# One step of an RWKV-7 and convolution layer: group norms with the tokens on the partitions, key norms folded into the scores, low-rank products on quarters of the array, the samples' convolution on TensorE, and the sample unit two places forward

## The chip, the cores and the metric

The kernel runs on one core of one Trainium2 chip. The metric is the device time of one execution in microseconds. Three executions were timed, and their median is the time of a kernel; one more was recorded by the profiler, and the views of the profile come from that one.

## What is computed

One layer over a prompt of 1024 tokens and over 8 samples of 4 tokens each, width 1024. Half of the mixing width goes through a recurrent branch (8 heads of 64), half through a causal convolution of 31 taps. Both read one input projection and end in one output projection. Cut to what matters here:

```python
h = _rms_norm(x, g_pre) * (1 + scale) + shift            # 1024 wide
u = h @ w_in                                             # r k v g w_lo a_lo | glu_a glu_b g_c
u_r = u_r + (u_prev - u_r) * mu                          # mix with the token before
w_log = -softplus(-(w0 + tanh(w_lo) @ w_up)) - 0.5       # low rank, 64 -> 512
a     = sigmoid(a0 + a_lo @ a_up)                        # low rank, 64 -> 512
kk = heads(k * k_k);  kk = kk / max(sqrt(sum(kk**2)), 1e-12)   # per token and head
# per token:  S = S diag(decay) - (S kk)(kk * a)^T + v k^T ;  y = S r
y   = group_norm(y, 8 heads)                             # 64 channels a group, per token
y_r = (y + bonus) * silu(g_r)
glu  = glu_a * sigmoid(glu_b)
conv = depthwise(concat(state_conv, glu), 31 taps) + b_dw
y_c  = silu(group_norm(conv, 8 groups)) * silu(g_c)
x + gate * _rms_norm(concat(y_r, y_c) @ w_out, g_post)
```

The states after the last token (recurrent, shift and convolution) are outputs too. The samples go through the same mathematics from given states.

## The kernel before

**Layout.** Between the projections everything lies with channels on the 128 partitions (two heads or two groups of 64) and tokens along the free dimension. The input projection runs in blocks of 128 output channels by 256 tokens: each is 8 slices of the contraction by three products in float32r (high part by high part, high by low, low by high), 24 instructions that write a tile `ps`. The output projection is the same with tiles `po`: 8 token blocks, each in two halves of 24 products (`JOBS`), the first half for the convolution's channels, the second for the recurrent branch's.

**Units.** The recurrent branch works in units of four heads (two channel blocks) by 128 tokens (256 columns): 16 units of the prompt, (0,0) to (1,7), and one of the samples (`SMP`). `ORDER` lists them. In a unit, `keys_unit` forms the low-rank products `zw` and `za` and the squares of the keys, `keys_unit2` norms the keys, `scores_unit` forms the products of queries and keys (`ap`), `blocks`, `solve`, `inverse` invert a small triangular matrix, `chain_unit` carries the state (tiles `cb`, `Yp`), `post_unit` norms the result. `chain_sample` and `post_sample` do this for the samples. The convolution branch goes by pieces of 128 channels by 256 tokens, 16 in all: `glu`, `shifts`, `convolutions` (tile `cv`), `post_conv`.

**The norms.** `inverse_norms` serves keys and both group norms. Two products (tile `n`, named `n2` in the code) sum the squares with the tokens on the partitions; VectorE applies the guard, GpSimd takes the power -1/2, ScalarE and GpSimd split it in two parts (`nR`, `nS`), two products turn it back (`n<-cs,nS`), ScalarE copies it (`nT`), and one product (`bc`) spreads it over the channels, where VectorE multiplies. A group norm has one product more ahead of this, which subtracts the mean (`yc`). So there are 17 norms of keys, 17 of the units' results and 16 of the convolution: 50 in all, 33 of them with `yc`.

**The samples' convolution** (`sample_block`) was four products over the taps per channel block on GpSimd, each summed by VectorE.

**What sets the order.** The whole program is recorded as strands and put into one order when it is built: `_Schedule.run` takes at each step the operation that can start first by a table of estimated costs (`_cost`), with the rank of its strand as tie break. On the chip each engine then works through its list in that order; SyncE (`Z`) issues nearly all DMAs, in its own list. `PLAN` sets the order of the projection's blocks (a lower case letter is the first half of the tokens, an upper case one the second). PSUM has six banks for most tiles: at most three of them (`room["pj"]`, `PJ = 3`) for `ps`, and at most four (`room["rest"]`) for all others, among them two for a `po` pair whose block number is not a multiple of three.

**The output weights** (`output_weights`) take the room that the normalised input had (`ha`, `hb`): the tiles `wo` are loaded, rounded by ScalarE and the rest is formed by GpSimd. `mixes` does the same with the mixed channels (`raw`, `mh`, `ml`).

Of the kernel before, what the change touches and what calls it, by code (L numbers as in the profile page):

```python
# [38 lines left out]
B1 A1 V2 A2 c0+ A3 g0+ c3 c1 g3 B3 C2 g2 G2 g1 C1 G1 G3 C3"""  # L39
# [11 lines left out]
ORDER = [(0, 0), (0, 1), (0, 2), (0, 3), (1, 0), (1, 1), (1, 2), (1, 3), (0, 4), (0, 5), (0, 6), (0, 7), (1, 4), (1, 5), (1, 6), (1, 7), SMP]  # L51
# [17 lines left out]
P_WDW = 57  # L69
P_GPRE = P_WDW + 4 * TAPS  # L70
# [237 lines left out]
class _Engine:  # L308
# [38 lines left out]
    def _cost(self, op, a, k):  # L347
# [3 lines left out]
        if self._n == "PE":  # L351
# [6 lines left out]
            if K == m == 64 and n == 128:  # L358
                return 0.065
            if a[1].dtype == F32R:  # L360
                return max(0.107, n * 0.00045)
# [43 lines left out]
def hymba_step(ctx, tc, xp, xs, cT, ssT, w_ada, badag, gpost, w_in, wup, par, cst, wkv, cvs, w_out, wdd,  # L405
# [14 lines left out]
    accd = tc.dram_tile([4, 128, 32], F32, name="accd")  # L420
    gld = [tc.dram_tile([128, 30 + SEQ], F32, name=f"gld{j}") for j in range(4)]
# [14 lines left out]
    hw = pr[:, P_WDW:P_WDW + 4 * TAPS]  # L436
    nR = const.tile([128, 19], F32, name="nR")
    half = nR[:, 18:19]
# [7 lines left out]
    heads4 = const.tile([68, 128], F32R, name="heads4")  # L446
# [8 lines left out]
    for i in range(3):  # L455
        for h in range(2):
            r, a = slice(32 * i, 32 * i + 4), C_ID + 32 * i + h
            V.tensor_tensor(heads4[r, 64 * h:64 * h + 64], cs[r, a:a + 1].to_broadcast([4, 64]),
                            cs[r, a + 2:a + 3].to_broadcast([4, 64]), ALU.add)
# [4 lines left out]
    sl = _Slots({"raw": 2, "ga": 2, "whi": WB, "wlo": WB, "qa": 4, "kb": 2, "unit": 2, "wd": 2, "sh": 2, "wa": 8, "ts": 1, "d2": 2, "dt": 1, "ti": 2}, sched)  # L464
# [79 lines left out]
    def modulation():  # L544
# [13 lines left out]
        for j in range(4):  # L558
# [3 lines left out]
            for i in range(KT // 2):  # L562
# [11 lines left out]
                if i == 1 and j == 0:  # L574
# [7 lines left out]
                    V.tensor_scalar(hw, hw, 0.5, None, ALU.mult)  # L582
# [227 lines left out]
    def output_weights():  # L810
        woh, wol = op["woh"], op["wol"] = {}, {}
        for ph in range(2):
            yield from wait(("proj", ph))
# [4 lines left out]
            jobs = [(4 - 4 * ph + k, q) for k in range(4) for q in range(2)]  # L818
            loaded, todo = [], jobs[:]
            for k, q in jobs:  # L820
                for tag in ("ga", "raw")[:1 + ph]:
                    while todo and sl.live[tag] < sl.bufs[tag]:
                        k_, q_ = todo.pop(0)
                        yield from sl.need(tag)
                        w = wp.tile([128, 512], F32, tag=tag, name="wo", bufs=sl.bufs[tag])
                        Z.dma_start(out=w, in_=w_out[k_ * 128:(k_ + 1) * 128, 512 * q_:512 * q_ + 512])
                        loaded.append((tag, w))
                if not loaded:
                    k_, q_ = todo.pop(0)
                    yield from sl.need("ga")  # L830
                    w = wp.tile([128, 512], F32, tag="ga", name="wo", bufs=sl.bufs["ga"])
                    Z.dma_start(out=w, in_=w_out[k_ * 128:(k_ + 1) * 128, 512 * q_:512 * q_ + 512])
                    loaded.append(("ga", w))
# [3 lines left out]
                G.tensor_tensor(wol[k][:, cc], w, woh[k][:, cc].bitcast(F32), ALU.subtract)  # L837
# [10 lines left out]
    def mixes():  # L848
        yield from wait("weights")
        for i, q in JOBS:  # L850
# [8 lines left out]
            G.tensor_tensor(ml, raw, mh.bitcast(F32), ALU.subtract)  # L859
# [107 lines left out]
    def gate(x, p, g, t):  # L967

        keys = [("z", ("c", p), g)] if x == "c" else [("z", p // 2, 2 * g), ("z", p // 2, 2 * g + 1)]
        n = UN + 32 * (x == "c" and g == NU - 1)  # L970
# [81 lines left out]
    def proj_conv(j):  # L1052
# [15 lines left out]
        def ev_c(g, ps, t):  # L1068
            for o, x in parts(t, ps, g):
                S.activation(o, x, AF.Tanh, scale=0.5)  # L1070
                V.scalar_tensor_tensor(o, o, 1.0, x, ALU.add, ALU.mult)
            gate("c", j, g, t)
# [28 lines left out]
    nT = cp1.tile([128, 288], F32R, name="nT")  # L1101
# [4 lines left out]
    def inverse_norms(nn, n, how, guard):  # L1106

        while not norms:
            yield BLOCK
# [700 lines left out]
    def taps_sample():  # L1810
        for j, ph in halves_of("ba"):
            if ph:
                yield from sample_block(j)
# [264 lines left out]
```

## Time and profile before

| | |
|---|---|
| timed executions | 866.39, 866.58 and 872.11 us; median 866.58 us |
| the profiled execution | 874.14 us, its span 872.4 us |
| TensorE busy | 815.5 us of the span |
| VectorE, ScalarE, GpSimd busy | 417.3, 462.8, 402.5 us |
| mean granted TensorE clock | 0.975 |

A span is the time from the first to the last instruction of the profiled execution. Most operations are recorded by one helper, so that the program's line says little (it is L341 nearly everywhere) and groups are told apart by the names of their tiles: `n<-cs,nS` writes tile `n` from `cs` and `nS`. A product in float32 is two instructions in the trace (x2), one in float32r is one. "PE" is the matrix product, "PEld" the load of its stationary operand. Busy time of a group of products is the union of spans that overlap, so what a product takes from the engine is better read as the distance from its start to that of the next instruction.

### The profile page before, as it was taken

How to read it: one execution, taken by the hardware profiler on the slowest of the kernel's cores; microseconds unless marked ns; L12 is line 12 of the kernel's file. 1: busy time of each engine (PE TensorE's matmuls, PEld its weight loads, DVE VectorE, ACT ScalarE, POOL GpSimd, SP SyncE). 2: the span in 40 equal slices, each digit the busy share in tenths (PEclk: the TensorE clock that was granted, in tenths of full speed). 3: DMA queues.
4: the chain of work that ended last, by engine and by line, in shares of the span. 5: the costliest groups of instructions: out<-in, count | busy, mean ns of one | idle time of the engine just before them, and what ended most of it. 6: DMA issues, size and time to landing. Idle time of an engine off the chain costs nothing.

```text
span 872.4 us, 23611 instructions
## 1 busy us (share of the span) xinstructions
PE 815.5 (93%) x9050; PEld 666.9 (76%) x9050; DVE 417.3 (48%) x1012; ACT 462.8 (53%) x1276; POOL 402.5 (46%) x759
## 2 busy tenths in 40 slices
PE   4868999999999999999999999999999999599995
PEld 2647888897889778888789878788987997475763
DVE  4556443562455554562662655574766363113122
ACT  4447577556676366672584567576655564211201
POOL 3237456463447216234325343644753765534332
PEclk9999899999999999999999999999999999698998
DMA  9987889788546753438735736435693676765432
GB/s 322 314 271 242 278 295 323 226 268 251 165 129 207 184 152 114 137 110 247 208 105 171 235 100 201 135 123 184 210 296 110 194 225 184 210 224 193 156 121 85
DMA packets 147729, 172.38 MB, mean 198 GB/s; under 512 B 23296, under 2 KB 105600, under 8 KB 147616
## 3 DMA queue, kind: packets, MB, share of 16 engines
q1 hardware_dynamic: 147328, 170.28, 63.0%
q8 instruction: 71, 1.16, 0.6%
q10 hardware_dynamic: 288, 0.59, 0.2%
q14 instruction: 42, 0.34, 0.1%
HBM read 112.68 MB, written 58.13 MB: 196 GB/s over the span
## 4 chain that ended last, share of the span: by engine, by line
PE 69%; DMA 14%; DVE 5%; ACT 4%; POOL 3%; issue 3%; SPq 1%; POOLq 0%; DVEq 0%; ACTq 0%
PE ps L341 30%; PE po L341 8%; PE cv L341 6%; PE n L341 4%; PE cb L341 4%; DMA wa<-w_ada 3%; PE ap L341 3%; PE Yp L341 2%; DMA xt<-xp 2%; PE yc L341 2%; PE p L341 2%; SPq L341 1%; PE bc L341 1%; DMA wd<-wdd 1%; ACT arena L341 1%
## 5 line engine op out<-in xcount | busy, mean ns | idle before, releaser
L341 PE MATMUL ps<-hb,whi 128*128 128x258 f32 (+3 forms) x928 | 199.0, 301 | 0.0
L341 PE MATMUL ps<-ha,whi 128*128 128x256 f32 (+2 forms) x864 | 180.9, 301 | 4.3 <-ACT ha L341 3.2
L341 PEld LDWEIGHTS ps<-hb,whi 128*128 128x128 f32 x928 | 149.6, 189 | 6.3 <-issue 2.7
L341 PEld LDWEIGHTS ps<-ha,whi 128*128 128x128 f32 x864 | 138.5, 191 | 14.8 <-issue 4.0
L341 PE MATMUL ps<-hb,wlo 128*128 128x258 f32 (+3 forms) x464 | 140.1, 302 | 0.0
L341 PE MATMUL ps<-ha,wlo 128*128 128x256 f32 (+2 forms) x432 | 130.9, 303 | 2.4 <-POOL wlo L341 2.4
L341 POOL TENSOR_TENSOR wlo<-raw,whi 128x512 fp32r<-128x512 f32 x58 | 78.4, 1352 | 66.1 <-ACT whi L341 50.2
L341 POOL TENSOR_TENSOR nR<-nR 128x4 f32<-128x4 f32 (+2 forms) x56 | 55.8, 998 | 77.5 <-DVE nR L341 77.2
L341 PEld LDWEIGHTS ps<-hb,wlo 128*128 128x128 f32 x464 | 87.6, 189 | 3.4 <-issue 1.2
L341 PEld LDWEIGHTS ps<-ha,wlo 128*128 128x128 f32 x432 | 82.4, 191 | 7.6 <-POOL wlo L341 3.0
L341 PE MATMUL cv<-SH,wd 128*32 128x256 f32 x1024 | 61.7, 389 | 4.0 <-DMA kept<-wlo 2.2
L341 ACT ACTIVATE arena<-ps,hp 128x256 f32<-128x256 f32 (+3 forms) x72 | 32.2, 455 | 51.7 <-PE ps L341 45.5
L341 ACT ACTIVATE X<-AB,cs 32x64 f32<-32x64 f32 x136 | 54.7, 403 | 2.1
L341 PEld LDWEIGHTS cv<-SH,wd 128*32 128x32 f32 x1024 | 35.1, 112 | 23.5 <-issue 2.7
L341 DVE SCALAR_TENSOR_TENSOR arena<-arena 128x256 f32<-128x256 f32 (+1 forms) x64 | 33.6, 527 | 34.3 <-DMA arena<-prj_a 13.1
L341 DVE TENSOR_TENSOR arena<-arena,bc 128x256 f32<-128x256 f32 (+2 forms) x50 | 20.6, 414 | 58.7 <-PE bc L341 56.2
L341 POOL TENSOR_TENSOR Ti<-Ti,tm 128x15 f32<-128x15 f32 (+4 forms) x135 | 41.1, 304 | 8.8
L341 ACT ACTIVATE whi<-raw 128x512 fp32r<-128x512 f32 x58 | 36.3, 626 | 15.6 <-DMA raw<-w_in 11.2
L341 POOL TENSOR_TENSOR tm<-D,Ti 128x15 f32<-128x15 f32 (+4 forms) x135 | 39.5, 293 | 10.2 <-DVE D L341 1.2
L341 ACT ACTIVATE arena<-arena 128x256 f32<-128x256 f32 (+3 forms) x100 | 41.1, 415 | 2.8 <-DVE ec L341 0.6
L341 DVE SCALAR_TENSOR_TENSOR arena<-ps,pr,arena 128x256 f32<-128x256 f32 (+4 forms) x40 | 17.5, 441 | 50.4 <-ACT arena L341 50.0
L341 POOL TENSOR_TENSOR arena<-arena,mx 128x256 f32<-128x256 f32 (+2 forms) x32 | 25.1, 785 | 35.3 <-ACT mx L341 31.8
(204 smaller groups left out, 1652.4 us busy)
## 6 DMA issues: line engine op xcount, KB each, us to landing
whi<-kept SPq DMA_DIRECT2D x52, 256.0 KB, 3.0
wlo<-kept SPq DMA_DIRECT2D x52, 256.0 KB, 3.8
raw<-w_in SPq DMA_DIRECT2D x50, 256.0 KB, 3.8
kept<-whi SPq DMA_DIRECT2D x44, 256.0 KB, 3.4
kept<-wlo SPq DMA_DIRECT2D x44, 256.0 KB, 3.2
wa<-w_ada SPq DMA_DIRECT2D x32, 256.0 KB, 5.4
SH<-gld SPq DMA_DIRECT2D x48, 142.0 KB, 4.0
xt<-xp SPq DMA_DIRECT2D x8, 512.0 KB, 5.4
```

The source lines that it names most:

```text
L341: emit = lambda: f(*a, **k)
```

## The change

- **Group norms in token layout.** `group_norm` turns the tile by `T.transpose` (tile `tp`, one per 128 tokens), so that the tokens lie on the partitions. VectorE sums each group, divides by 64, subtracts; ScalarE squares; VectorE sums; GpSimd adds the guard, takes the power and multiplies; two more transposes turn it back (tile `yc`). The products `yc` with `bcen`, `n` and `bc` are gone.
- **Key norms.** `square_sums` forms the sum of squares of each key with the keys' position on the partitions: eight products of a 64x64 stationary operand and one column (`n<-cs,arena 64x1`). The keys are no longer multiplied. Instead the reciprocal of the square norm (`inv`) goes into the scores' first half (`AB`, on VectorE, where ScalarE copied it before) and into `MV` in `chain_unit` and `chain_sample`: there one instruction of ScalarE over 64x128 becomes two over 64x64, each with a scale per partition, and VectorE multiplies by a tensor instead of by -1.
- **Low-rank products on quarters.** `zw` and `za` of the prompt's units: four products of 64x128 stationary operands become eight of 64x64, each with its place in the array.
- **The samples' convolution on TensorE.** `glu_sample` writes the samples' columns to memory, `shifts` loads them four times shifted and `convolutions` runs 32 products of 32 columns per channel block, with the weights of the prompt's last piece. `post_conv_sample` norms and gates all four blocks at once. The products over the taps on GpSimd and their sums on VectorE are gone, as are the weights for them (`hw`).
- **Order.** `SMP` stands two places ahead of the end in `ORDER`; `B3` three places further ahead in `PLAN`.
- **Output weights.** The loads of the second half may start once the last weights are in, ahead of the last projection; every second low part of that half, and all `ml`, are formed by VectorE instead of GpSimd.
- Two of the planner's estimated costs are raised a little.

```diff
-B1 A1 V2 A2 c0+ A3 g0+ c3 c1 g3 B3 C2 g2 G2 g1 C1 G1 G3 C3"""
+B1 A1 V2 A2 c0+ A3 B3 g0+ c3 c1 g3 C2 g2 G2 g1 C1 G1 G3 C3"""
-ORDER = [..., (1, 4), (1, 5), (1, 6), (1, 7), SMP]
+ORDER = [..., (1, 4), (1, 5), SMP, (1, 6), (1, 7)]
...
+    def square_sums(nn):
+        n2 = yield from bank([128, NCH], "n2")
+        for u in range(NCH):
+            for h in range(2):
+                T.matmul(n2[H[h], u:u + 1], nn[H[h], 64 * u:64 * u + 64], cs[H[h], C_ONE + 64 * h:C_ONE + 64 * h + 1],
...
+        V.tensor_scalar(t, n2, 1e-24, None, ALU.max)
...
+            for a in range(2):
+                w = slice(128 * i + 64 * a, 128 * i + 64 * a + 64)
+                for x, z in enumerate((zw, za)):
+                    T.matmul(z[H[a], cc], wu[H[x], w], tw[H[x], c0:c0 + 128], start=True, stop=True, tile_position=(64 * x, 64 * a))
...
-                S.activation(AB[H[h], :, 0, :], aps[h][H[h], :, 0:64], AF.Copy)
+                V.tensor_tensor(AB[H[h], :, 0, :], aps[h][H[h], :, 0:64], iv(h), ALU.mult)
...
-            S.activation(mv[H[0], :, c, 0, :], cb[H[0], 1], AF.Copy, scale=-1.0)
-            V.tensor_scalar(mv[H[1], :, c, 1, :], cb[H[1], 1], -1.0, None, ALU.mult)
+            for i, u in slots:
+                S.activation(MV[H[0], u, 0, :], cb[H[0], 1, i], AF.Copy, scale=inv[H[0], i, c:c + 1])
+            V.tensor_tensor(mv[H[1], :, c, 1, :], cb[H[1], 1], inv[H[1], :, c].unsqueeze(2).to_broadcast([64, 2, 64]), ALU.mult)
...
     def group_norm(src, n, guard):
-        T.matmul(yc[:, :n], bcen, src, start=True, stop=True)
...
-        bc = yield from inverse_norms(q, n, ALU.add, guard)
-        V.tensor_tensor(q[:, :n], src, bc[:, :n], ALU.mult)
...
+        for i, w in tiles:
+            T.transpose(tp[0:w, i, :], src[:, 128 * i:128 * i + w], ident)
...
+            V.tensor_reduce(a, by_group(tp, ii, w), mybir.AxisListType.X, ALU.add)
+            V.tensor_scalar(a, a, 1.0 / 64, None, ALU.mult)
+            V.tensor_tensor(by_group(qv, ii, w), by_group(tp, ii, w), spread(a), ALU.subtract)
+            S.activation(sq[0:w, ii], qv[0:w, ii], AF.Square, scale=0.125)
+            V.tensor_reduce(b, by_group(sq, ii, w), mybir.AxisListType.X, ALU.add)
+            G.tensor_scalar(b, b, 1.0, guard, ALU.mult, ALU.add)
+            G.tensor_tensor(b, b, half[0:w].unsqueeze(2).to_broadcast([w, m, 2]), ALU.pow)
+            G.tensor_tensor(by_group(qv, ii, w), by_group(qv, ii, w), spread(b), ALU.mult)
...
+        for i, w in tiles:
+            T.transpose(yc[:, 128 * i:128 * i + w], qv[0:w, i, :], ident[0:w, 0:w])
...
-            G.tensor_tensor(ml, raw, mh.bitcast(F32), ALU.subtract)
+            V.tensor_tensor(ml, raw, mh.bitcast(F32), ALU.subtract)
-                G.tensor_tensor(wol[k][:, cc], w, woh[k][:, cc].bitcast(F32), ALU.subtract)
+                (V if ph and q else G).tensor_tensor(wol[k][:, cc], w, woh[k][:, cc].bitcast(F32), ALU.subtract)
...
+                x = sh[:, :, 4 * m:4 * m + UN]
+                if g == NU:
+                    x = sh[:, :, 0:NB * 34].rearrange("p c (b x) -> p c b x", x=34)[:, :, :, 4 * m:4 * m + 4]
```

What this moves on the engines is shown at three places.

TensorE in the first third of the program, before: a norm's last products (`n<-cs,nS`, then `bc`) around a convolution, the low-rank product `zw` with its stationary operand of 128 columns, and the mean's product `yc` of another norm.

```order
L341 MATMUL n_2770<-cs,nS 4x128 x2
L341 MATMUL cv<-SH,wd 32x256 x28
L341 MATMUL bc<-nT,heads_126 128x256
L341 MATMUL p_2852<-TS,AB 32x32 x16
L341 MATMUL zw<-tw,wu 128x128 x2
L341 MATMUL yc<-arena,cs 128x256
L341 MATMUL ps<-ha,whi 128x256
```

TensorE in the same part, changed: one unit's low-rank products in turn on quarters, and behind them the two transposes that open a group norm.

```order
L340 MATMUL zw<-tw,wu 64x128
L340 MATMUL za<-tw,wu 64x128
L340 MATMUL zw<-tw,wu 64x128
L340 MATMUL za<-tw,wu 64x128
L340 MATMUL tp<-cs,arena 128x128 x2
L340 MATMUL ps<-hb,whi 128x258 x2
L340 MATMUL ps<-hb,wlo 128x258
```

`zw` and `za` now stand together, and of a norm's four kinds of products two are left, `tp` and `yc`.

TensorE in the middle, changed: the samples' convolution of one channel block (`cv` with 32 columns, which has no counterpart on TensorE before), between the state's products (`cb`, `Yp`) and another norm's transposes.

```order
L340 MATMUL cb<-MV,Q 64x64 x4
L340 MATMUL Yp<-Q,MV 64x64 x4
L340 MATMUL cv<-SH,wd 32x32 x32
L340 MATMUL cb<-Wt,TT 64x64 x4
L340 MATMUL p_6212<-T_6142,AB 32x32 x8
L340 MATMUL tp<-cs,arena 128x128 x2
```

These 32 products are now in TensorE's list four times, once per channel block.

TensorE behind the last `ps`, before: the group norm of the samples (160 columns in two parts), with the output projection `po` around it.

```order
L341 MATMUL yc<-arena,cs 128x160
L341 MATMUL po<-ha,mh 128x512 x2
L341 MATMUL po<-ha,ml 128x512 x2
L341 MATMUL n_10932<-cs,arena 128x2
L341 MATMUL n_10932<-cs,arena 32x2
L341 MATMUL n_10932<-cs,nS 4x128
L341 MATMUL n_10932<-cs,nS 4x32
L341 MATMUL bc<-nT,heads_126 128x160
L341 MATMUL po<-ha,mh 128x512 x2
```

TensorE behind the last `ps`, changed: the samples' convolution norm (one `tp`) and the last norm of a unit (`tp` x2), then three transposes back in a row.

```order
L340 MATMUL tp<-cs,arena 128x128
L340 MATMUL po<-ha,mh 128x512 x2
L340 MATMUL po<-ha,ml 128x512 x2
L340 MATMUL po<-ha,mh 128x512 x4
L340 MATMUL po<-ha,ml 128x512 x2
L340 MATMUL tp<-cs,arena 128x128 x2
L340 MATMUL po<-ha,mh 128x512 x4
L340 MATMUL po<-ha,ml 128x512 x2
L340 MATMUL yc<-cs,arena 128x128 x3
L340 MATMUL po<-ha,mh 128x512 x2
L340 MATMUL po<-ha,ml 128x512
```

Before, the four small products `n` and `bc` stood with no `po` among them; now six `po` stand between the last `tp` and the three `yc`. The samples' state products (`sp`, `cb`, `Yp`, `mp`), which before stood among the `po`, are all ahead of the last `ps` now.

More of the change, by code (lines that the diff above doesn't have):

```diff
@@ L812, in output_weights, with load @@
         for ph in range(2):
+            jobs = [(4 - 4 * ph + k, q) for k in range(4) for q in range(2)]
+            loaded, todo = [], jobs[:]
+            def load():
+                for tag in ("ga", "raw")[:1 + ph]:
+                    while todo and sl.live[tag] < sl.bufs[tag]:
+                        k, q = todo.pop(0)
+                        yield from sl.need(tag)
+                        w = wp.tile([128, 512], F32, tag=tag, name="wo", bufs=sl.bufs[tag])
+                        Z.dma_start(out=w, in_=w_out[k * 128:(k + 1) * 128, 512 * q:512 * q + 512])
+                        loaded.append((tag, w))
+            if ph:
+                yield from wait("weights")
+                yield from load()
             yield from wait(("proj", ph))
@@ L817, in output_weights @@
                 woh[4 - 4 * ph + k], wol[4 - 4 * ph + k] = t[:, k], t[:, 4 + k]
-            jobs = [(4 - 4 * ph + k, q) for k in range(4) for q in range(2)]
-            loaded, todo = [], jobs[:]
             for k, q in jobs:
[L821 to L833, printed above, removed]
+                yield from load()
+                while not loaded:
+                    yield BLOCK
+                    yield from load()
                 tag, w = loaded.pop(0)
@@ L1130, in inverse_norms @@
         drop(n2)
-        yield
-        bc = yield from bank([128, 512], "bc")
-        T.matmul(bc[:, 0:n], heads4[rows], nT[rows, 0:n], start=True, stop=True)
-        sched.later(lambda: norms.append(x))
-        return bc
+        return t
     def keys_unit(p, g):
@@ L1725, in gating @@
             name, p, g, _, t = x
[L1726 removed]
+            n = UN
             row = p + 4 * (name == "c")
@@ L1844, in post_conv, with swish @@
+    def swish(z, q, yc, gains):
+        for cc, a, b in gains:
+            S.activation(z[:, cc], yc[:, cc], AF.Identity, scale=a, bias=b)
+        n = gains[-1][0].stop
+        drop(yc)
+        S.activation(q[:, 0:n], z[:, 0:n], AF.Tanh)
+        V.scalar_tensor_tensor(z[:, 0:n], q[:, 0:n], 1.0, z[:, 0:n], ALU.add, ALU.mult)
     def post_conv(first, step):
@@ L1919, in outputs_sample @@
     def outputs_sample():
-        yield from wait("gates", ("y", 0, NE - 1), ("y", 1, NE - 1), ("mix", SMP), *(("mix", ("c", k), NU - 1) for k in range(4)))
+        yield from wait("gates", ("y", 0, NE - 1), ("y", 1, NE - 1), ("mix", SMP), ("mix", "cs"))
         m = yield from take("nt", "m")
```

266 lines of the change are left out of this document (130 added, 136 removed).

## The prediction

> **What bounds the kernel now.** I read the page's busy times first, then the busy time of each engine by stage, then TensorE's timeline, the waits and the chain of waits.
>
> ```profile
> span 872.4 us, 23611 instructions
> PE 815.5 (93%) x9050; PEld 666.9 (76%) x9050; DVE 417.3 (48%) x1012; ACT 462.8 (53%) x1276; POOL 402.5 (46%) x759
> 0.00:109.00 109.00, 82.92 (x696) 64.34 (x697) 57.61 (x122) 56.90 (x132) 46.36 (x70) 0.95 0.88 286
> 109.00:723.10 614.10, 606.52 (x7638) 514.21 (x7638) 322.70 (x825) 375.06 (x1066) 295.85 (x615) 1.00 0.63 190
> 723.10:862.30 139.20, 125.92 (x720) 88.32 (x718) 34.86 (x64) 29.59 (x76) 57.59 (x71) 0.93 0.52 167
> 862.30:872.40 10.10, 0.10 (x1) 0.00 (x0) 2.10 (x3) 1.27 (x4) 2.71 (x4) 0.67 0.45 157
> PE 69%; DMA 14%; DVE 5%; ACT 4%; POOL 3%; issue 3%; SPq 1%; POOLq 0%; DVEq 0%; ACTq 0%
> ```
>
> The four rows by stage give the stretch and its length, then the busy time of PE, PEld, DVE, ACT and POOL, the granted TensorE clock, the DMA share and GB/s. I put the bounds where TensorE's work changes kind. In the front (to 109 us) TensorE idles 26 us and the DMA share is 0.88: transfers pace it. In the middle (109 to 723.1, where the last `ps` ends) TensorE is busy 606.5 of 614.1 us at full clock, and no other engine above 375. In the tail (`po`) it idles 13.3 us (139.2 - 125.9). In the last 10.1 us it has nothing to do. TensorE holds 69% of the chain that ended last. So for 753 us the time is a sum over TensorE's instructions, and an edit is worth what it takes from or gives to that list.
>
> **Price of a product.** TensorE's products overlap in the records, so I take as price of a group the distance from its start to that of the next group. The columns are start, duration, operation and count.
>
> ```profile
> 728.50 0.70 PE L341 MATMUL yc<-arena,cs 128*128 128x256 f32 x2
> 728.85 0.58 PE L341 MATMUL po<-ha,ml 128*128 128x512 f32 x1
> ...
> 730.29 0.39 PE L341 MATMUL bc<-nT,heads 4*128 4x288 f32 x1
> 730.62 0.61 PE L341 MATMUL n<-cs,arena 128*128 128x2 f32 x4
> 731.08 0.71 PE L341 MATMUL po<-ha,ml 128*128 128x512 f32 x2
> ...
> 733.79 2.04 PE L341 MATMUL sp<-Q,M 64*64 64x16 f32 x64
> 735.76 0.60 PE L341 MATMUL n<-cs,nS 128*4 128x128 f32 x4
> 736.29 0.51 PE L341 MATMUL po<-ha,mh 128*128 128x512 f32 x1
> ```
>
> *Norms, removed.* `yc` 0.35 (728.85 - 728.50), `bc` 0.33, the sums `n` 0.46, the way back `n<-cs,nS` 0.53 us. A group norm gives up all four, 1.67 us; a key norm the last three, 1.32 us. The program has 33 and 17 of them: 33 x 1.67 + 17 x 1.32 = **-77.5 us**.
>
> ```profile
> 117.55 0.71 PE L341 MATMUL za<-tw,wu 64*128 64x128 f32 x4
> 118.18 0.39 PE L341 MATMUL ps<-ha,whi 128*128 128x256 f32 x1
> ...
> 190.80 1.58 PE L341 MATMUL ap<-Q,KB 64*64 64x128 f32 x32
> 192.32 0.50 PE L341 MATMUL ps<-ha,whi 128*128 128x258 f32 x2
> ...
> 340.57 1.22 PE L341 MATMUL ap<-Q,KB 64*64 64x128 f32 x32
> 341.72 0.41 PE L341 MATMUL ps<-hb,wlo 128*128 128x298 f32 x1
> 586.81 0.60 PE L341 MATMUL kt<-cs,KB 128*128 128x128 f32 x4
> 587.24 0.38 PE L341 MATMUL vt<-cs,arena 128*128 128x128 f32 x2
> 587.38 0.38 PE L341 MATMUL ps<-hb,wlo 128*128 128x298 f32 x1
> 704.85 0.45 PE L341 MATMUL p<-TS,AB 32*32 32x32 f32 x32
> 705.23 0.54 PE L341 MATMUL ps<-hb,whi 128*128 128x298 f32 x2
> ```
>
> *Low-rank products.* A unit's `za` takes 118.18 - 117.55 = 0.63 us, and with a `zw` of the same shape it is 1.26 us in 8 instructions. On quarters they are 16 instructions with 128 columns each. The nearest row is `ap`, also quarters with 128 columns: 1.52/32 = 47 ns and 1.15/32 = 36 ns. I take 44: 16 x 0.044 = 0.70 us. Over 16 units that is **-8.9 us**; -10.9 at 36 ns, and 0 if the quarters don't overlap and each instruction takes as long as one of today's divided by two, 79 ns.
>
> *Key sums, added.* 17 units x 8 products x 2 instructions = 272, each with a 64x64 stationary operand and one column. The nearest row is `sp` (64x64, 16 columns): 1.97/64 = 31 ns, so **+8.4 us**. Below it lies `p` (32x32), 0.38/32 = 12 ns: 3.3; above it `ap`, 47 ns: 12.9. The Trainium skill, "TensorEngine Tiling (Array Packing)", section "Instruction Overhead", says that one column costs as much as 60, about 60 cycles, which speaks against sums of one column at a time; at the 2.4 GHz of "TensorE: Matmul & The Clock Gate" that is an estimate of 25 ns an instruction, and +6.8 us in place of 8.4. `p` at 12 ns is under that where products of different quarters overlap, as far as this trace goes.
>
> *Transposes, added.* 32 norms of 256 columns with two `tp` and two `yc` each, one norm with four of the samples' results and one with two of their convolution: 134 in all. `kt` (128x128, a transpose too) takes 0.43/4 = 107 ns: **+14.3 us**. The ends: `vt`, 0.14/2 = 70 ns, 9.4 us; `n<-cs,nS` (128 columns), 0.53/4 = 133 ns, 17.8 us.
>
> *The samples' convolution, added.* 4 blocks x 32 products x 2 instructions = 256, with a stationary operand of 128x32.
>
> ```profile
> L341 PE MATMUL ada<-wa,sc 128*32 128x128 f32 x256 | 12.7, 306 | 14.5 <-DMA wa<-w_ada 14.5
> L341 PE MATMUL cv<-SH,wd 128*32 128x256 f32 x1024 | 61.7, 389 | 4.0 <-DMA kept<-wlo 2.2 <-DMA wd<-wdd 1.7 <-issue 0.2
> ```
>
> Same stationary operand: `ada` 12.7/256 = 50 ns (128 columns), `cv` 61.7/1024 = 60 ns (256 columns). With 32 columns it can be less, `sp`'s 31 ns. I take 50: **+12.8 us** (7.9 to 15.4). Its transfers (a store and four shifted loads a block, in SyncE's list) I cost at nothing, because the block waits in a stretch where TensorE has `ps` to do; if the cover is gone, it is a landing or two, of the size of the tail term below.
>
> The sum of TensorE's list is -77.5 - 8.9 + 8.4 + 14.3 + 12.8 = **-50.9 us**; with all low ends -67.8, with all high ends -31.4. The samples' state products, which now stand ahead of the last `ps`, change place, not this sum.
>
> **Waits and clock.** The tail's waits, and two stretches of it with their clock (column after POOL):
>
> ```profile
> 752.15 0.59 PE L341 MATMUL n<-cs,nS 128*4 128x128 f32 x2 [5.42 <-POOL nS L341]
> 756.23 0.27 PE L341 MATMUL n<-cs,nS 32*4 32x32 f32 x2 [3.49 <-POOL nS L341]
> 749.70:763.40 13.70, 7.38 (x19) 5.25 (x20) 2.00 (x6) 2.42 (x6) 6.47 (x8) 0.50 0.69 209
> 797.50:804.30 6.80, 6.57 (x16) 4.75 (x17) 5.49 (x9) 0.00 (x0) 3.88 (x6) 0.50 0.34 101
> ```
>
> The samples' norm stops TensorE for 5.42 and 3.49 us, since no product stands between its steps; the other 4.4 us of the idle are short. In the new order the first is spread among `po` and the second stands ahead of the last `ps`: **-13.3 us**, the whole idle of the tail. What is late next is the three `yc` in a row, behind only six `po` from the last `tp`. The chain between them is priced by these groups (count, busy time, mean in ns, idle before).
>
> ```profile
> L341 DVE TENSOR_REDUCE accs<-arena 128x8 f32<-128x248 f32 x16 | 6.5, 406 | 6.0 <-POOL arena L341 5.9
> L341 DVE TENSOR_SCALAR nR<-n 128x4 f32<-128x4 f32 x48 | 7.7, 161 | 30.3 <-PE n L341 29.4 <-POOL nS L341 0.2
> L341 DVE TENSOR_TENSOR arena<-arena,bc 128x256 f32<-128x256 f32 x44 | 18.2, 416 | 51.2 <-PE bc L341 50.8
> L341 POOL TENSOR_TENSOR nR<-nR 128x4 f32<-128x4 f32 x48 | 50.1, 1044 | 77.5 <-DVE nR L341 77.2
> L341 POOL TENSOR_TENSOR TT<-T,cs 128x256 f32<-128x256 f32 x17 | 11.5, 678 | 30.2 <-DVE T L341 30.2
> L341 POOL TENSOR_TENSOR ml<-raw,mh 128x512 fp32r<-128x512 f32 x16 | 20.8, 1297 | 28.9 <-ACT mh L341 27.5 <-PE po L341 1.4
> PE bc L341 <- ACT nT L341: 0.4, 1, 0.4
> 815.82 21.38 PE po L341 x91
> ```
>
> Two reductions 0.41 each, the division 0.16, the subtraction 0.42, the square (256 columns on ScalarE, taken as the same 0.42), GpSimd's small addition (0.16 as well), its power 1.04 and its product 0.68: 3.7 us without queues. One GpSimd instruction of `ml`'s size may stand ahead (1.30; the formation of `hb`'s low parts is queued there), and eight hand-offs at 0.15 (an estimate, under the 0.4 of the one wait for `nT`) are 1.2: 6.2 us. Six `po` (21.38/91 = 0.235 us each) cover 1.4: **+4.8 us**; without queue and hand-offs 2.3. Behind these `yc` stands the next `po`, which can't pass them in TensorE's list.
>
> The two stretches at clock 0.50 hold 7.38 and 6.57 us of TensorE's work, which full clock would halve: **-7.0 us**; after the new wait I put one such stretch back, **+3.0**. In the middle I add **+3** for small new waits (a norm, or a landing), and in the front TensorE waits for transfers, so that what is removed there gains nothing: **+2**.
>
> Off the path: VectorE loses the multiplication by `bc` and gains reductions, subtractions, `AB` and `ml` (at most the 20.8 us of GpSimd); 33 norms x (2 x 0.41 + 0.16 + 0.42) = 46 less 18.2 and 7.7, with 13 for `AB`, leaves it near 470 of 815 us, 58%. GpSimd and ScalarE lose work. No engine comes near the length. `PLAN`, the estimated costs and the earlier `wo` loads alter the order only: I cost them at nothing while TensorE's list stays full.
>
> The sum: 872.4 - 50.9 - 13.3 + 4.8 - 7.0 + 3.0 + 3 + 2 = 814.0 us of span. The profiled execution took 874.14, 1.74 beyond its span: 815.7. The median of the timed runs is 866.58, 0.9914 of it: **809 us**.
>
> **The rivals.**
>
> *Forecast*, with the ends of TensorE's list (-67.8 to -31.4): 792 to 828. Chance 0.53. For it: full clock and 98.8% busy in the middle.
>
> *Better*: no wait at `yc`, none in the middle, no half clock again (-10.8), and small products at their low ends (-16.9): 781; with half of the latter, 790. For it: products of one column are the smallest in the program. Against: the new norm is a chain of eight instructions over three engines. Chance 0.18.
>
> *The norm's chain is longer than its cover in the middle*, about 1 us in each of 30 norms: 809 + 30 = 839. Against: the old chain had the power and two crossings more, and the waits inside a norm that have a row above are one of 0.4 us for `nT` and the two for `nS` in the samples' norm. For it: the new one puts 0.68 us of GpSimd and 0.42 of VectorE between `tp` and `yc`, where only small tensors passed before. Chance 0.13.
>
> *Something else sets the middle's length*, the state's chain for one (it gets two ScalarE instructions for one in each step): TensorE's freed time turns to waiting, and only the tail gains. By the code it has 384 `po`, 90 us, and some 14 us of others: 872.4 - 35 = 837 of span, 832 us. Against: TensorE idles 7.6 us in 614, so nothing there shows a second bound; but so full an engine would hide one. Chance 0.09.
>
> *Slower*: GpSimd's queue. The new chain passes GpSimd three times, and each pass can stand behind one instruction of 1.3 us (`ml`'s size): 3.7 + 1.2 + 3.9 = 8.8 us. If the order keeps 6 us of products between `tp` and `yc` as a rule, every one of 33 norms stops TensorE 2.8 us: +92 us, less the 3 already counted: 898 us. It decides from (866.6 - 809)/33 = 1.8 us a norm. Half clock would sharpen it: the second stretch at 0.50 has TensorE idle for only 0.23 of 6.80 us. The Trainium skill, "TensorE: Matmul & The Clock Gate", Part 1, gives half clock after an idle window of about 3.4 us; by that rule a short wait costs itself alone and this rival stays smaller; the stretch at 797.5 differs, with no such idle time inside it, and the measurement decides. Against this rival: GpSimd was busy 46% and gets less work; and the old norms, which passed it with the same power, stopped TensorE in the middle by less than its 7.6 us of idle time, all together. Chance 0.07.
>
> **The numbers.** About 1%, 8.7 us, is what a measurement of this kernel can tell from no change. Faster by over 1% (under 857.9) are the first four but for 0.02 at the long end of the norm's chain: 0.91; within 1%: 0.02; slower by over 1%: 0.07. The range 784 to 845 takes the forecast, nearly all of *better*, the two cases at 832 and 839 and leaves out *slower* and parts of the ends.
>
> **What would show it.** TensorE's busy time near 760 us; no `n<-cs,nS` and no `bc`; the last `ps` near 695 us of the span and 105 to 110 us of `po` behind it; waits of TensorE for `yc` only behind the last `ps`, of some 5 us; full clock in the tail but for one stretch; `zw` and `za` of one unit in 0.7 us; 32 products of the samples' `cv` in about 3.2 us. The step on the norm is wrong if the waits show `yc` in many places in the middle; that on TensorE's list, if its busy time falls by less than 31 us; the frame itself, if the idle time of TensorE grows by as much as its work falls.

## The result and the profile after

The changed kernel takes 822.11 us (median of 819.24 to 825.62) against 869.35 us for the kernel before, with one more run of it than was known ahead: a ratio of 0.944, 95% interval 0.936 to 0.953. The forecast was 809 us in a range of 784 to 845. The profiled execution took 821.62 us, where the sum of terms gave 815.7.

The page of the changed kernel, and its windows, with the front cut at 109 us as before and the middle ending where the last `ps` ends (columns as in the windows of before):

```profile
span 819.8 us, 24132 instructions
PE 752.2 (92%) x9308; PEld 629.1 (77%) x9308; DVE 453.8 (55%) x1110; ACT 426.3 (52%) x1147; POOL 362.3 (44%) x721
PE 53%; DMA 21%; SPq 7%; DVE 6%; ACT 3%; issue 3%; POOL 2%; DVEq 0%; ACTq 0%; POOLq 0%
0.00:109.00 109.00, 84.60 (x765) 65.28 (x766) 55.76 (x114) 58.51 (x135) 44.20 (x69) 0.97 0.87 285
109.00:699.90 590.90, 567.05 (x8092) 488.59 (x8090) 356.34 (x922) 339.61 (x945) 282.59 (x602) 1.00 0.69 206
699.90:809.30 109.40, 100.25 (x460) 75.21 (x458) 39.56 (x73) 26.87 (x65) 32.50 (x46) 0.97 0.59 184
809.30:819.80 10.50, 0.30 (x2) 0.00 (x0) 2.10 (x3) 1.27 (x4) 2.99 (x5) 0.62 0.40 151
```

TensorE's work fell by 63.3 us (815.5 to 752.2) and the span by 52.6, so 10.7 us came back as idle time of TensorE: 56.9 us before, 67.6 now. The windows say where. In the middle it idles 23.9 us (590.90 - 567.05), where it was 7.6; in the tail 9.2, where it was 13.3; in the front 24.4, where it was 26.1. (A wait of 2.5 us at `adg`, for weights of the front, now ends behind the cut at 109 us and counts to the middle.) The chain that ended last runs through TensorE for 53%, not 69%, and through DMA and SyncE's queue for 28%.

The longer waits of TensorE in the changed kernel behind the front (us in total, times, longest), and the row of all `cv`, whose idle time (11.9 us) stands behind the second bar:

```profile
L340 PE MATMUL cv<-SH,wd 128*32 128x256 f32 (+1 forms) x1280 | 61.6, 344 | 11.9 <-DMA SH<-gld 5.9
PE cv L340 <- DMA SH<-gld: 5.9, 4, 2.5
PE yc L340 <- POOL arena L340: 5.0, 2, 3.6
PE cv L340 <- DMA wd<-wdd: 2.9, 3, 1.4
PE adg L340 <- DMA wg<-w_ada: 2.8, 3, 2.2
PE cb L340 <- ACT MV L340: 2.5, 5, 0.8
PE po L340 <- DMA arena<-mixd: 2.5, 1, 2.5
PE ps L340 <- ACT KB L340: 2.0, 1, 2.0
PE po L340 <- DMA wo<-w_out: 1.7, 1, 1.7
PE Yp L340 <- ACT MV L340: 1.4, 3, 0.9
PE cb L340 <- DVE MV L340: 0.9, 1, 0.9
```

The wait for `yc` is the one that was forecast. The waits at `cv` (10.7 of the 11.9 us for transfers) and at `po`, and those for `MV` in the state's chain, are the ones that were not.

### The profile page after: what moved, and what is told of

The parts are those of the page before. It is cut to its first block, busy times and chain, and to the rows that moved or that the text cites. A ratio compares the mean times of both kernels' runs of the same rounds, so it can differ in the third digit from the quotient of the medians.

```text
span 819.8 us, 24132 instructions
## 1 busy us (share of the span) xinstructions
PE 752.2 (92%) x9308; PEld 629.1 (77%) x9308; DVE 453.8 (55%) x1110; ACT 426.3 (52%) x1147; POOL 362.3 (44%) x721
## 4 chain that ended last, share of the span: by engine, by line
PE 53%; DMA 21%; SPq 7%; DVE 6%; ACT 3%; issue 3%; POOL 2%; DVEq 0%; ACTq 0%; POOLq 0%
PE ps L340 24%; PE po L340 7%; SPq L340 7%; PE cv L340 5%; PE cb L340 4%; DMA arena<-prj_a 3%; DMA SH<-gld 2%; DMA gld<-arena 2%; PE Yp L340 2%; DVE arena L340 2%; DMA raw<-w_in 2%; PE p L340 2%; PE ap L340 2%; DMA wo<-w_out 1%; DMA raw<-mixd 1%
## 5 line engine op out<-in xcount | busy, mean ns | idle before, releaser
L340 PE MATMUL ps<-hb,whi 128*128 128x298 f32 (+3 forms) x928 | 197.3, 301 | 0.0
L340 PE MATMUL ps<-hb,wlo 128*128 128x258 f32 (+3 forms) x464 | 138.3, 298 | 0.0
L340 PE MATMUL cv<-SH,wd 128*32 128x256 f32 (+1 forms) x1280 | 61.6, 344 | 11.9 <-DMA SH<-gld 5.9
L340 DVE SCALAR_TENSOR_TENSOR arena<-arena 128x256 f32<-128x256 f32 (+1 forms) x66 | 29.9, 453 | 73.9 <-DMA arena<-prj_a 26.1
L340 PEld LDWEIGHTS cv<-SH,wd 128*32 128x32 f32 x1280 | 39.1, 110 | 29.3 <-issue 9.7
L340 ACT ACTIVATE whi<-raw 128x512 fp32r<-128x512 f32 x58 | 36.4, 628 | 26.1 <-DMA raw<-w_in 15.7
L340 ACT ACTIVATE arena<-arena 128x256 f32<-128x256 f32 (+4 forms) x103 | 41.3, 409 | 16.5 <-DVE arena L340 12.2
L340 POOL TENSOR_TENSOR arena<-arena,mx 128x256 f32<-128x256 f32 (+2 forms) x32 | 24.4, 763 | 34.6 <-ACT mx L340 25.4
L340 PE MATMUL po<-ha,mh 128*128 128x512 f32 x128 | 38.0, 416 | 0.0
L340 POOL TENSOR_TENSOR st<-st,half 128x4 f32<-128x4 f32 (+2 forms) x35 | 35.3, 1008 | 2.2
```

The source lines that it names most:

```text
L340: emit = lambda: f(*a, **k)
```

## The experiments

Each run is the changed kernel with the one edit shown, cut to its main lines; the ratio is to the kernel before, run beside it. The kernel before had medians from 868.64 to 874.42 us in these groups of runs, so a difference of a few us between two groups says little by itself.

The granted clock differs from trace to trace too. Behind the front, TensorE works 8.9 us at clock 0.50 in the trace of the changed kernel (115.6 to 119.0 us, and 5.5 us of work from 716.3 to 723.1). Where another trace has much more of it, this is said.

### Group norms in the channel layout again

```diff
-    q, yc = group_norm(...)    # tp, sums on VectorE, yc
+    q = group_norm(...)        # yc with bcen, n, n<-cs,nS, bc
```

> The group norms alone go back to the channel layout (products yc, n, n<-cs,nS and bc); everything else stays as changed. Theory (the time is the sum of TensorE's list): 33 x 1.67 = 55 us of products return, the 19 us of transposes tp and yc go, so TensorE's busy time rises by about 36 us to 788, and the time by 27 to 38 us, to 849 to 860 us; the less, the more of the 21.6 us that TensorE idles between 120 and 700 us is filled by the extra products. Rival (something else now sets the middle's length): TensorE's idle time falls by more than 15 us and the time rises by no more than 20 us.

863.69 us, ratio 0.989 (0.983 to 0.995): 41.6 us more than with the change. Its page:

```profile
span 862.8 us, 24584 instructions
PE 800.5 (93%) x9544; PEld 661.0 (77%) x9544; DVE 429.7 (50%) x1045; ACT 453.7 (53%) x1249; POOL 338.1 (39%) x686
```

TensorE's work rises by 48.3 us, the span by 43.0: the idle time falls only from 67.6 to 62.3 us. The theory holds, at 4 us above its upper end; the rival, a second engine that sets the middle's length, asked for at least 15 us less idle and falls. About 7 of the 48.3 us are the clock: this trace has 22.6 us of TensorE's work at 0.50, in place of 8.9. Taken back alone, the group norms cost 41.6 of the 47 us. All else in the change together leaves 869.03 - 863.69 = 5.3 us.

### The low-rank products on whole rows again

```diff
-    for a in range(2): T.matmul(z[H[a], cc], ... 64 columns ..., tile_position=(64 * x, 64 * a))
+    T.matmul(z[:, cc], wu[H[x], 128 * i:128 * i + 128], tw[H[x], c0:c0 + 128])
```

> Only zw and za of the prompt's units go back to stationary operands of 128 columns, 8 instructions a unit. Theory: TensorE's list grows by what the two traces show between them, about 4.7 us (17.1 us of zw and za before, 12.4 now, by the advance of TensorE's front), or by 8.9 us as the prediction priced it; the time follows, 824 to 831 us. Rival: the quarters gain nothing, and the time stays within 3 us of 822.

822.55 us, ratio 0.943 (0.935 to 0.951): no difference. One unit's products, first in the changed kernel (from 130.55 to the next product at 131.19 us, 16 instructions, those between left out), then in this run:

```profile
130.55 0.32 PE L340 MATMUL zw<-tw,wu 64*64 64x128 f32 x1
...
131.19 0.39 PE L340 MATMUL ps<-ha,wlo 128*128 128x256 f32 x1
```

```profile
214.14 0.37 PE L340 MATMUL zw<-tw,wu 64*128 64x128 f32 x1
214.15 0.37 PE L340 MATMUL za<-tw,wu 64*128 64x128 f32 x1
214.35 0.27 PE L340 MATMUL zw<-tw,wu 64*128 64x128 f32 x1
...
214.58 0.27 PE L340 MATMUL za<-tw,wu 64*128 64x128 f32 x1
214.82 0.45 PE L340 MATMUL d<-P,TS 32*32 32x32 f32 x32
```

0.64 us on quarters; 0.68 us on halves, once `zw` and `za` of one unit stand in turn: each starts within 0.01 us of the other. Before, in the unit that the forecast priced, they stood apart and took 0.64 and 0.63 us. Where they stand in turn, the quarters add nothing to that. In this run 15 of the 16 units have them in turn and one has them apart. Before the change, seven of the 16 stood in turn already.

### The power of each group norm twice

```diff
+    G.tensor_tensor(a, b, half, ALU.pow)      # a is not read any more
     G.tensor_tensor(b, b, half, ALU.pow)
```

> GpSimd forms the power of each group norm twice, the first into a place that is not read; the order on all engines is that of the changed kernel. Each of 33 norm chains gets about 1.04 us longer. Theory (the chain is hidden in the middle and open in the tail): TensorE's wait for yc in the tail grows from 5.0 to about 6 to 7 us, no wait for yc in the middle above 1 us in sum, the time rises by 1 to 4 us. Rival (the chain is as long as its cover in the middle): a wait at most norms, 20 to 31 us more.

828.64 us, ratio 0.951 (0.944 to 0.958): 6.5 us more, above the 1 to 4 expected and far from 20 to 31. The order is the same on all engines, so the waits can be compared:

```profile
PE yc L349 <- POOL arena L349: 9.9, 7, 4.5
```

It was 5.0 us in two waits; of the 4.9 us more, 1.4 lie in the middle in all its norms together, the rest in the tail. The norms are hidden in the middle and open in the tail, as the forecast had it; this run adds that most of those in the middle have a microsecond to spare. What the 6.5 us hold besides these waits is not shown.

### The state's chain longer

```diff
     for i, u in slots:
         S.activation(MV[H[0], u, 0, :], cb[H[0], 1, i], AF.Copy, scale=inv[...])
+        S.activation(MV[H[0], u, 0, :], cb[H[0], 1, i], AF.Copy, scale=inv[...])   # again
```

> In the state's chain of the prompt each of the two ScalarE instructions that write MV from cb is issued twice; the order is that of the changed kernel. Each of 32 steps gets about 0.6 us longer (two of 308 ns by their row, less what overlaps). Theory (TensorE's list sets the length, the state's chain has other products beside it): TensorE's waits for MV grow from 4.8 us to about 10, the time by 3 to 8 us. Rival (the state's chain sets the middle's length): 13 to 20 us more.

843.39 us, ratio 0.967 (0.960 to 0.975): 21.3 us more, the rival's size and a little over it. The waits for `MV`, and one window of this run:

```profile
PE cb L349 <- ACT MV L349: 10.7, 19, 1.5
PE Yp L349 <- ACT MV L349: 1.9, 5, 0.5
PE cb L349 <- DVE MV L349: 1.6, 5, 0.5
360.00:365.00 5.00, 4.46 (x33) 3.62 (x34) 1.74 (x6) 2.74 (x10) 0.00 (x0) 0.50 0.11 11
```

They grow from 4.8 to 14.2 us, most of them under 1 us. From the start of the first instruction that writes `MV` to the end of the last, a step now takes 1.72 us in place of 1.05 (medians of the 32 steps): 21 us in all, the size of what the time lost.

Not all of it shows as waiting. In this profile (838.38 us, the shortest of the four runs) TensorE's idle time is 6.1 us longer than in the changed kernel (73.7) and its busy time 10.7 us (762.9). Part of the latter is clock 0.50: here, at 335 to 345 us behind a wait of 1.5 us, and at 500 to 510 us behind one of 3.0 us at `cv`; 21.7 us of work at that clock behind the front, in place of 8.9, cost 6.4 of the 10.7 us. The run with the output weights loaded late (below) has the changed kernel's order on all engines, and 18.8 us of work at that clock without a longer chain. Against its trace, 11.8 of the 15.2 us more are idle time. So the waits are the larger part, and the clock blurs how large.

Together with the first run this says something that neither theory had: extra work in TensorE's list lengthens the time, and so does extra length of the state's chain, each by about its own size. Both can be so because each engine works through a fixed list: a step that comes later than the list was made for stops TensorE at that place, whatever stands behind it.

### Without the samples' convolution

```diff
-    Z.dma_start(out=gsm[j], in_=t)             # shifted loads and 64 products a block follow
+    Z.dma_start(out=accd[j], in_=t[:, 0:32])
```

> The samples' convolution is left out: no shifted loads and no products of 32 columns for the samples, and the norm behind it works on the samples' inputs instead; the rest stays. Theory (the 256 products cost 12 ns each, and TensorE's waits for transfers at cv come from the prompt's own round trip through memory): TensorE's list falls by 3.1 us, its waits at cv stay at 9 us or more of 11.9, the time falls by 2 to 5 us. Rival (the samples' transfers in SyncE's list hold up the prompt's): the waits at cv fall to 4 us, as before the change, and the time by 8 to 11 us.

815.38 us, ratio 0.936 (0.928 to 0.943): 6.7 us less, between the two. TensorE's waits at `cv` fall from 11.9 to 6.5 us. A block's 64 products had taken 0.69 us in the changed kernel (420.35 - 419.66), 11 ns each:

```profile
419.66 0.76 PE L340 MATMUL cv<-SH,wd 128*32 128x32 f32 x64
420.35 0.45 PE L340 MATMUL cb<-Wt,TT 64*64 64x64 f32 x8
```

### The samples' convolution on GpSimd again

```diff
-    for j, g, ph in with_samples():            # in shifts and convolutions
+    for j, g, ph in pieces():
+    G.tensor_tensor(prod, windows(GS[:, b:b + 2, :]), wj, ALU.mult)     # as before the change, and VectorE's sums
```

> Only the samples' convolution goes back: four products over the taps per block on GpSimd with VectorE's sums, none on TensorE and no shifted loads for it; the samples' norm behind it stays as changed. Theory (this part of the change costs time, since it puts 3.1 us on TensorE and its transfers ahead of the prompt's cv, while the old way lay on engines that are half idle): as where the convolution was left out, 5 to 8 us less than the changed kernel, 814 to 817 us, with waits of TensorE at cv near 6 us. Rival (GpSimd's 11 us and VectorE's 6.5 us push the chains that TensorE waits for): the gain is under 2 us or gone.

821.46 us, ratio 0.941 (0.936 to 0.946): no difference, and the waits at `cv` are 14.6 us, although the shifted loads are gone here too. The rival holds: what leaving the work out had saved doesn't come back by moving it to GpSimd. This part of the change neither gains nor costs what can be measured.

### The samples' unit last

```diff
-ORDER = [..., (1, 5), SMP, (1, 6), (1, 7)]
+ORDER = [..., (1, 5), (1, 6), (1, 7), SMP]
```

> Only ORDER goes back: the samples' unit stands last. Theory (the samples' chain needs products beside it, which the tail lacks): its state products and its norm come back behind the last ps, with waits of TensorE in the tail of 8 to 13 us above the changed kernel's 9.2, and the time rises by 5 to 13 us. Rival (the new norm without the way through n and bc hides there as well): no more than 3 us.

827.09 us, ratio 0.948 (0.942 to 0.954): 5.0 us more, the theory's low end, all four runs (from 826.08) above all of the changed kernel's (to 825.62). By the ratios (0.948 and 0.944) the intervals overlap. And the waits of the tail are 8.3 us, not 17 to 22: all waits for `yc` are 2.8 us, where the samples' norm before the change stopped TensorE for 8.9. In the profile the 5 us are not waits at all:

```profile
PE 765.0 (93%) x9308; PEld 638.3 (77%) x9308; DVE 455.3 (55%) x1110; ACT 426.3 (52%) x1147; POOL 362.4 (44%) x721
```

TensorE's idle time is 60.1 us, 7.5 less than in the changed kernel, and its busy time 12.8 us longer, with 24.1 us of work at clock 0.50 behind the front in place of 8.9. The theory's mechanism did not show, and what the place of the samples' unit is worth stays open.

### The output weights loaded late again

```diff
-            if ph:
-                yield from wait("weights")
-                yield from load()
             yield from wait(("proj", ph))
```

> The loads of the second half of the output weights start only behind the last projection again; the division of their low parts between VectorE and GpSimd stays. Theory: the loads' landing (about 4 us and the chain to hb behind it) comes in the tail, where TensorE has only po: 1 to 5 us more of waits at po, the time rises by 1 to 5 us. Rival: the loads are hidden by the first po in any case, no change beyond 2 us.

820.59 us, ratio 0.940 (0.933 to 0.946): no difference; the rival holds. TensorE's list is the same as in the changed kernel, row by row, so this pair also shows how far two programs of one order differ: 1.5 us in the medians, and 18.8 against 8.9 us of work at clock 0.50 behind the front of their traces.

### Transfers reckoned slower when the order is made

```diff
-            end = self.dma + 2.2
+            end = self.dma + 4.2
```

> One number of the planner: it reckons with 4.2 us from the end of a transfer's turn to its data in place of 2.2; the work is the same, the order differs. Theory (TensorE stands at cv because the order puts cv ahead of the landing that the chip gives, 4 to 6 us): the waits for transfers at cv fall from 11.9 us to under 6, and the time by 4 to 8 us. Rival (the transfers themselves set the middle's length by now): the waits turn up elsewhere, and the time stays within 3 us of 822.

835.89 us, ratio 0.958 (0.951 to 0.965): 13.8 us more. The first half of the theory came true, since no wait at `cv` is left; the time did not follow. Work now stands later, and the tail from the last `ps` (685 us) is 137 us long in place of 110, with new waits:

```profile
PE po L340 <- DMA wo<-w_out: 7.0, 1, 7.0
PE yc L340 <- POOL arena L340: 4.3, 1, 4.3
PE 766.0 (92%) x9308; PEld 636.7 (76%) x9308; DVE 459.2 (55%) x1110; ACT 422.2 (51%) x1147; POOL 367.6 (44%) x721
```

Yet the waits are not the loss. TensorE's idle time fell by 12.2 us in the middle and rose by 8.7 in the tail and 2.1 in the front; in all it is 66.3 us, where the changed kernel has 67.6. Its busy time is 13.8 us longer (766.0 against 752.2), with 31.1 us of work at clock 0.50 behind the front in place of 8.9: 11 of the 13.8 us. All four runs show a lower mean clock, 0.953 to 0.963, where the changed kernel has 0.977 to 0.985. Why this order gets it is not shown.

### Both halves of `MV` on VectorE

The timeline of one step of the state's chain shows why it is long. Before the change (VectorE's row, then ScalarE's), and after it (ScalarE's two rows, then VectorE's):

```profile
451.99 0.29 DVE L341 TENSOR_SCALAR MV<-cb 64x128 f32<-64x128 f32 x1 [0.33 <-PE cb L341]
452.32 0.27 ACT L341 ACTIVATE MV<-cb 64x128 f32<-64x128 f32 x1 [0.75 <-DVE MV L341]
```

```profile
507.82 0.31 ACT L340 ACTIVATE MV<-cb,er 64x64 f32<-64x64 f32 x1 [0.31 <-PE cb L340]
508.50 0.31 ACT L340 ACTIVATE MV<-cb,er 64x64 f32<-64x64 f32 x1 [0.36 <-DVE MV L340]
508.17 0.29 DVE L340 TENSOR_TENSOR MV<-cb,er 64x128 f32<-64x128 f32 x1 [1.62 <-ACT MV L340]
```

The three write different parts of `MV`, and yet each starts when the one before has ended: 0.99 us from 507.82 to 508.81, where it was 0.60 (451.99 to 452.59). The row stands so in 23 of the 32 steps; in the other nine ScalarE's two stand together, and most of these steps take 0.84 to 0.95 us. The medians are 1.05 us now and 0.67 before; over 32 steps that is some 11 us of chain.

What makes the row is not settled. Parts of `MV` as such can be written by two engines at once, as a few microseconds later, where VectorE (to 513.31) and GpSimd (from 513.13) both write it:

```profile
512.84 0.47 DVE L340 COPY MV<-Mo 64x128 f32<-64x128 f32 x2
513.13 0.90 POOL L340 TENSOR_TENSOR MV<-MV,er 64x128 f32<-64x128 f32 x2 [1.13 <-DVE MV L340]
```

The instructions of the row also read one tile, `cb`, and nowhere in this trace do two engines read `cb` at the same time. No run separates the two.

```diff
-            for i, u in slots:
-                S.activation(MV[H[0], u, 0, :], cb[H[0], 1, i], AF.Copy, scale=inv[H[0], i, c:c + 1])
-            V.tensor_tensor(mv[H[1], :, c, 1, :], cb[H[1], 1], inv[H[1], :, c]..., ALU.mult)
+            for h in range(2):
+                V.tensor_tensor(mv[H[h], :, c, h, :], cb[H[h], 1], inv[H[h], :, c]..., ALU.mult)
```

> In the state's chain of the prompt VectorE writes both halves of MV, two instructions one behind the other, in place of ScalarE, VectorE and ScalarE again, which the trace shows one after the other (0.31, 0.29, 0.31 us with two changes of engine) though they write different places. Each of 32 steps gets about 0.4 us shorter. Theory (a step of the state's chain that takes longer than the order allows stops TensorE at its place): the inverse of the run with the instructions doubled (0.6 us a step, 17 to 21 us): TensorE's waits for MV fall from 4.8 us to under 2, and the time by 5 to 12 us. Rival (in the changed kernel the chain has slack but for those 4.8 us; only making it longer costs): 1 to 4 us less.

813.56 us, ratio 0.934 (0.929 to 0.939): 8.6 us less, and all six runs (808.54 to 818.12) lie below all four of the changed kernel. Its waits at `MV` and the two longest kinds at `cv` (7.1 us in all, in place of 11.9):

```profile
PE cv L340 <- DMA wd<-wdd: 3.6, 4, 1.7
PE cb L340 <- DVE MV L340: 1.7, 1, 1.7
PE cv L340 <- DMA SH<-gld: 1.6, 3, 0.8
```

The wait named `MV` here is one, ahead of `cb<-MV,Q`; those behind the edited instructions are gone. TensorE's idle time falls by 7 us in the middle (from 120 us on) and 3 in the tail. The order changed with the edit, so that the shorter chain and the other order can't be told apart in this run; the run with doubled instructions, in one order, can be read that way.

### Two combinations

The first takes the edits of GpSimd's convolution and of `MV` together.

> Both of the edits before it: samples' convolution on GpSimd, both halves of MV on VectorE. If the two gains are in different waits they add up, 802 to 812 us; if both only fill the same idle time of TensorE, the time is that of the better of the two.

818.60 us, ratio 0.941 (0.937 to 0.946): neither of the two that were expected, 5.0 us above `MV` alone. Here the last `ps` stands at 659 us and part of the convolution behind it (4.1 us of waits at `cv` in the tail, and one of 7.6 us at `po` for `mixd`): another order again.

The second takes that of `MV` with this:

```diff
-    (V if ph and q else G).tensor_tensor(wol[k][:, cc], w, woh[k][:, cc].bitcast(F32), ALU.subtract)
+    (V if ph else G).tensor_tensor(wol[k][:, cc], w, woh[k][:, cc].bitcast(F32), ALU.subtract)
```

> Both halves of MV on VectorE, and all low parts of the second half of the output weights formed by VectorE (0.68 us each) in place of every second one on GpSimd (1.31 us each), where two of them stand ahead of the last norm's steps. Theory: TensorE's wait for yc in the tail, 5.0 us in the changed kernel and 2.3 with MV alone, falls to under 1.5, and the time by 1 to 3 us, to 811 to 813 us. Rival (VectorE's own queue, which has the norm's sums and subtraction too, takes its place): the wait stays or grows, the time 814 or above.

814.47 us, ratio 0.937 (0.933 to 0.941): no gain over `MV` alone; the wait for `yc` is 3.0 us, not under 1.5. The rival holds.

## Why the prediction was right, and where it was off

The frame held: the time is the sum over TensorE's list, plus its waits. The terms, as forecast and as the trace has them; the price of a group over a whole run is the part of each record that no record with an earlier end covers, summed.

- *Norms removed, -77.5.* The four groups of before sum to 77.4 us that way (`n` 21.4, `n<-cs,nS` 24.7, `yc` 16.8, `bc` 14.5). Right.
- *Transposes, +14.3.* `tp` 9.0 and `yc` 10.2: 19.2 us. Above the upper end of 17.8; 143 ns each, more than any row it was priced by, `kt` at 107 among them.
- *Key sums, +8.4.* 9.1 us, 34 ns each. Right. The estimate by the Trainium skill, "TensorEngine Tiling (Array Packing)", section "Instruction Overhead", was 6.8, at 25 ns; this trace shows more for a single column on a 64x64 quarter.
- *Samples' convolution, +12.8.* 4 blocks of 0.69 us: 2.8. Mis-sized, under even the low end of 7.9: the 11 ns are those of `p`, 32 columns on 32 of the array's columns, four side by side, and not those of `ada` with 128 columns. Its transfers, costed at nothing, were not free in the run without the samples' convolution: TensorE waits 5.4 us less at `cv` there. In the run with GpSimd the waits stay without them, so how much of the waits is theirs stays open.
- *Low-rank products, -8.9.* 17.1 us before and 12.4 now: -4.7, inside the bounds of -10.9 and 0. The reason given was wrong: the run on whole rows has 13.0 us of them and the same time, so what there is comes from `zw` and `za` standing in turn, not from quarters. And the forecast priced all 16 units by one whose two stood apart, where seven of them stood in turn already.

In sum these five are where the forecast had them (-51.0 against -50.9), and that is luck: the convolution's error, -10, is offset by +4.9, +4.2 and +0.7. TensorE's busy time came out 8.4 us lower than the 760.6 that the sum implies. The difference lies in `ps`, `po` and `ap`, whose number did not change; why they took less is not shown.

The waits are where the sum was off. *Tail, -13.3 and +4.8*: the old idle went, and the three `yc` wait 5.0 us, with a low part of `hb` (1.26 us) ahead of the last norm's steps in GpSimd's list, as forecast. Not forecast were 4.2 us at `po` for `mixd` and `wo`. *Half clock, -7.0 and +3.0*: one stretch is left in the tail, from within the longer wait for `yc`; it costs 2.8 us, half of the 5.5 us of work in it:

```profile
716.00:718.00 2.00, 0.42 (x3) 0.42 (x3) 0.51 (x2) 1.26 (x2) 1.92 (x3) 0.58 0.70 201
718.00:720.00 2.00, 2.00 (x7) 1.57 (x6) 1.69 (x4) 0.63 (x1) 0.76 (x1) 0.50 0.73 232
720.00:722.00 2.00, 2.00 (x6) 1.51 (x6) 0.12 (x1) 0.00 (x0) 0.00 (x0) 0.50 0.67 204
722.00:724.00 2.00, 2.00 (x8) 1.59 (x7) 0.00 (x0) 0.00 (x0) 0.00 (x0) 0.72 0.26 59
```

*Middle, +3 for small new waits*: this is the step that failed. The idle time there grew by 16.3 us (23.9 - 7.6). The main parts are 7.9 us more at `cv` (11.9, where it was 4.0), 4.8 at `MV`, 2.5 at `adg` from the front, and 2.0 at `ps` for `KB`. So the list was full and stood still all the same, at places where transfers and the state's chain cross into it. The step "they alter the order only: I cost them at nothing while TensorE's list stays full" rests on the same idea; of its three parts only the earlier loads were undone, and they make no difference. No run undid `B3` in `PLAN` or the estimated costs. In the front the forecast lost 2 us; idle time fell by 1.7, or rose by 0.8 with the wait at `adg` counted there.

Of the span's miss, 5.8 us (819.8 against 814.0), +13 is the middle's idle time, +4 the tail's, -4 the front's, -8 TensorE's work. The other 7 us of the 13 between 809 and 822 come from the last step, the factor 0.9914 between one profiled execution of before and the median of three; in the changed kernel the profiled execution (821.62) is the median but for 0.5 us.

Of the rivals, *the norm's chain longer than its cover* and *slower* are excluded by the run with the doubled power. *Something else sets the middle's length* is excluded in the form given, by the run with the old norms; what it named, the state's chain with two ScalarE instructions for one, was the right place with the wrong mechanism. Its price was taken as one instruction more; it is one more in a row of three on two engines, each of which waits for the last.

That the fold of the key norms gives back most of its gain in TensorE's list (17 x 1.32 - 9.1 = 13 us) through this chain is argued only, from the 5.3 us that are left and from the 8.6 us of the `MV` edit; no run undid the fold alone, and it stays open. Why the waits at `cv` grew from 4.0 to 11.9 us is not settled either: they move with every order (5.4 to 14.6 us in the runs that have them), and the one order without them had no less idle time in all and lost by the lower clock.

## What to carry to other kernels

Where one engine is busy 98% and its list is fixed, price a change twice: by what it does to the list, and by what it does to each chain that crosses into the list, since a step 0.4 us later than planned costs up to 0.4 us at each of its places. Look in the timeline at instructions of two engines that write parts of one tile, or read parts of one: if each starts when the other ends, they are a row, not a pair. Price a small product by a row with about as many moving columns: `p` (32 columns, 12 ns) fitted the samples' convolution, `ada` (128 columns, 50 ns) did not. And when two runs differ by a few us, split the difference into idle time and busy time, and look at the granted clock, before it is put down to a wait.

## What the runs showed of the hardware that was not expected

Products of 32 columns with stationary operands of 128x32 took 11 ns each when four stand side by side (0.69 us for 64), where those with 128 columns took 50 ns. Here the price fell with the moving columns, while the key sums with a single column kept 34 ns. 16 of them, up to the start of the next product:

```profile
122.39 0.63 PE L340 MATMUL n<-cs,arena 64*64 64x1 f32 x16
122.95 0.39 PE L340 MATMUL ps<-ha,wlo 128*128 128x258 f32 x1
```

The granted clock fell to 0.50 for some 6 us around 360 us in the run with the longer state's chain, with no wait there above 0.5 us but several within 5 us, and 0.11 of the DMA engines busy:

```profile
358.99 0.36 PE L349 MATMUL Yp<-AB,MV 64*64 64x64 f32 x1 [0.24 <-ACT MV L349]
360.06 0.58 PE L349 MATMUL Yp<-AB,MV 64*64 64x64 f32 x5 [0.37 <-ACT MV L349]
361.65 0.47 PE L349 MATMUL zw<-tw,wu 64*64 64x128 f32 x1 [0.47 <-ACT arena L349]
```

So the half clock that the forecast had read off the tail of before, behind waits of under 1 us, is not peculiar to the tail.
